# Two transformer blocks on one core: the halves of each buffer of FFN intermediates 1152 bytes apart instead of 1024

## The chip, the cores and the metric

The kernel runs on one core of a Trainium2 chip. The metric is the device time of one execution in microseconds (us), the median of three runs. All sizes in bytes below are bytes within one partition of SBUF, unless something else is said.

## The reference, cut to what matters

The program computes two blocks one after the other on 256 tokens of width 1024, in float32. The first block has two layers. Each layer has two feed-forward networks (FFNs), so there are four: f00, f01, f10 and f11 by their names in the kernel.

```
def swiglu(x, w_gu, w_down):
    gate, up = jnp.split(x @ w_gu, 2, axis=-1)     # w_gu 1024 x 5632, w_down 2816 x 1024
    return (jax.nn.silu(gate) * up) @ w_down

h = h + 0.5 * rmsnorm(swiglu(rmsnorm(h, g[0]), ffn_w_gu[l, 0], ffn_w_down[l, 0]), g[1])
```

Between the FFNs of layer 0 stands a gated convolution, between those of layer 1 a differential attention. The second block has a sparse attention, a state-space branch, and a mixture of 32 experts with 2 chosen for each token. The change touches the first block alone.

## The kernel before, in words

**Float32 products in three matmuls.** Each operand is split into a high part (hi), which ScalarE rounds to TensorE's fast float32 form, and a low part (lo), the rest, which VectorE subtracts. A product is then three matmuls that accumulate in PSUM: hi·hi, hi·lo and lo·hi. Weights come by DMA in units of 512 KB (4096 bytes per partition, tile `raw`), line 170 makes `hi`, line 175 makes `lo`. They lie in nine pairs of slots, a to f and x to z.

**One FFN.** `Ffn.body` (line 613) goes through the 2816 hidden columns in 11 pieces of 256.
- For a piece, `wstat` (line 485) makes the gate `g`, and a second call the up part `u`. Each is 48 matmuls of 256 columns: the weights are stationary and the transposed activations `xTh`, `xTl` are moving. Lines 491, 492 and 493 take turns.
- ScalarE takes silu of `g`, VectorE multiplies by `u`, and `split` (line 400) writes the result as the pair `hTh`, `hTl`. Each of these tiles holds two halves, hidden columns 0 to 127 and 128 to 255 of the piece, 256 tokens each. They come from the pool `hp` with four buffers for the high and four for the low parts.
- `rows` (line 498) then multiplies an older piece by its two units of `w_down`. Here the halves of `hTh` and `hTl` are stationary, 128 tokens at a time, and 512 columns of the weights are moving. The loop is over the halves outside and the token halves inside, so a block is 12 matmuls on half 0 and then 12 on half 1, into four PSUM banks `fo`. Lines 392, 393 and 394 (`mm3`) take turns.

So the steady order on TensorE is 48 matmuls of `g`, 48 of `u`, a block of 24 of `fo`, and again. In f00, f01 and f11 the first two pieces are made token-stationary (`fq`, lines 392 to 394) while the norm of the second token half is still running, and there are blocks at pieces 2 to 8; pieces 9 and 10 have none. In f10 there are blocks at pieces 1 to 7. That is 7 blocks for each FFN. The last four pieces of `fo`, the tail, are multiplied in `boundary` (line 506): for the first token half, for each PSUM bank, piece by piece, both halves in turns of 3 matmuls; for the second token half 6 matmuls for each half.

Other products with 512 moving columns, which the prediction uses for comparison, are `co` and `ao` (the convolution and attention of block one, whose stationary tiles `yT` and `oT` lie in the same pool `hp`), and `wa` and `ws` in block two (stationary tiles `oTh0` to `oTl1`, and `yTh`, `yTl` from other pools). `xb` and `tk` are products of block two in the manner of `g` and `u`, and of `fq`.

**Where the tiles lie.** The allocator of the built program gives these first bytes, and the remainder by 256 in the last column:

| tiles | first byte in a partition | mod 256 |
|---|---|---|
| weights, slots a to f | 56832, and on by 4096 | 0 |
| weights, slots x to z | 168704, and on by 4096 | 0 |
| `xTh`, `xTl` | 212928, 221120 | 192 |
| `hTh`, `hTl`, eight buffers, half 0 | 152320, and on by 2048 | 0 |
| the same, half 1 | 1024 further | 0 |
| `oTh0`, `oTh1`, `oTl0`, `oTl1` (for `wa`) | 140160, and on by 4096 | 128 |
| `yTh` for `ws` (two of four groups) | 111936, 107840 | 64 |
| `yTl` for `ws` (the same groups) | 157440, 136064 | 0, 128 |

All steps inside a weight tile, 1024 or 2048 bytes, and inside `xT`, 1024 bytes, are multiples of 256. So are the steps to the second half of the columns or tokens, 512 bytes. What remains of a tile's first byte is therefore that of every stationary or moving piece taken from it.

The order on each engine is made by a scheduler from the program and its priorities.

Of the kernel before, what the change touches and what calls it, by code (L numbers as in the profile page):

```python
# [9 lines left out]
F32R = mybir.dt.float32r  # L10
# [6 lines left out]
P = 128  # L17
T = 256
# [14 lines left out]
B_Q, B_K, B_IK, B_DT, B_AL, B_LAM, B_DS, B_RT, B_END = 0, 64, 128, 192, 224, 256, 512, 544, 580  # L33

UNIT = 1024
TAIL = 4
CHUNKED = 2
BEHIND = 4
# [38 lines left out]
class Weights:  # L77
# [21 lines left out]
    def raw_of(self, i):  # L99
        k = (i - self.base) % self.nr  # L100
        for pool, n in reversed(self.raws):
            k -= n
            if k < 0:
                break
        return pool.tile([P, UNIT], F32, name=f"raw{i}", tag="raw")

# [41 lines left out]
    def step(self):  # L148
# [7 lines left out]
        self.free.remove(s)  # L156
        hi = self.pools[s].tile([P, UNIT], F32R, name=f"hi{i}", tag=f"hi{s}")
        lo = self.pools[s].tile([P, UNIT], F32R, name=f"lo{i}", tag=f"lo{s}")
        self.slot[i] = s
# [62 lines left out]
def kernel(ctx: ExitStack, tc: tile.TileContext, a: dict, out: bass.AP, upto=99, start=1):  # L222
# [18 lines left out]
    def banks4(name):  # L241
        return [[accp.tile([P, 512], F32, name=f"{name}{i}{j}", tag=f"acc{i}{j}") for j in range(2)] for i in range(2)]
# [5 lines left out]
    def add_piece(w, c0):  # L248
        return [W.add(cols(w, c0, c0 + 256, k, k + 4)) for k in (0, 4)]

    def add_rows(w, k0, n=2):
        return [W.add(cols(w, 0, D, k, k + 1)) for k in range(k0, k0 + n)]

    def add_ffn(l, j, chunked):
        gu, dn = a["ffn_w_gu"][l, j], a["ffn_w_down"][l, j]
        g, u, d = [], [], []
        for n in range(FT // 2):
            g.append(add_piece(gu, n * 256))
            u.append(add_piece(gu, DFF + n * 256))
            if chunked <= n < FT // 2 + chunked - TAIL:  # L260
                d.append(add_rows(dn, 2 * (n - chunked)))
        d += [add_rows(dn, FT - 2 * n) for n in range(TAIL, 0, -1)]
        return g, u, d
# [82 lines left out]
    hp = blk1.enter_context(tc.tile_pool(name="hp", bufs=4))  # L346
# [37 lines left out]
    def scr(name, dt=F32):  # L384
        return sc.tile([P, 512], dt, name=name, tag="sc")


    def hot(n=HOT):
        return tc.high_priority(offset=n)
# [40 lines left out]
    def post_norm(i, acc, g, factor):  # L430
        ss = mean_square(acc[i], D)
        t = two.tile([P, D], F32, name="t", tag="t")
        for j in range(2):
            dve.scalar_tensor_tensor(halves(t)[j], acc[i][j], factor, halves(g)[j], op0=ALU.mult, op1=ALU.mult)
        r = rstd_of(ss[:, 0:1], ss[:, 1:2])
        for j in range(2):
            dve.scalar_tensor_tensor(halves(h[i])[j], halves(t)[j], r, halves(h[i])[j], op0=ALU.mult, op1=ALU.add)
# [68 lines left out]
    def boundary(tail, acc, post, nxt, first=False, pooled=POOLED, at=AT, behind_tr=LEFT):  # L506

        for j in range(2):
            for n, (p, lT) in enumerate(tail):
                m = rows(0, p, lT, acc, first and n == 0, n == len(tail) - 1, js=(j,))  # L510
        with hot():
            post(0)
            nxt.pre(0)
        if BEHIND_PRE:
            W.behind(BEHIND_PRE)
        for u in range(W.split, min(W.split + 16, len(W.src))):
            if (u - W.split) in pooled:
                W.on_pool.add(u)
        W.cut = 2
        late[0] = m  # L520
        left = 2 * len(tail)
        for n, (p, lT) in enumerate(tail):
            for m in range(2):
                rows(1, p, lT, acc, first and n == 0, n == len(tail) - 1, m, m + 1)
                left -= 1
                if left == behind_tr:
                    with hot():
                        late[0] = nxt.tr(0)
                    W.behind(BEHIND)
            W.done(*p, pump=left > behind_tr)  # L530
        late[0] = None
        with hot():
            post(1)
        seen = [0]

        def piece_done():
            seen[0] += 1
            if seen[0] == at:
                with hot():
                    nxt.pre(1)  # L540
                    late[0] = nxt.tr(1)
                W.behind(BEHIND)

        at = nxt.at or at
        hook[0] = piece_done
        nxt.chunk(0)
        hook[0] = late[0] = None
        if seen[0] < at:
            seen[0] = at - 1
            piece_done()  # L550
            late[0] = None
        W.cut = 1
        nxt.chunk(1)
# [30 lines left out]
    class Ffn(Phase):  # L584
# [4 lines left out]
            self.chunked = chunked  # L589

        def new_lT(self):
            t = tuple(hp.tile([P, 2, T], F32R, name=f"hT{p}", tag=f"hT{p}") for p in "hl")
            self.lT.append(t)
            return t

# [17 lines left out]
        def body(self, nxt):  # L613
            x = xT[self.key]
            acc = None
            np_ = FT // 2
            for n in range(self.chunked, np_):
                g_ps = bank("g")
                wstat(x, self.gp[n], g_ps)
                hd = scr("hd")  # L620
                act.activation(hd, g_ps, AF.Silu)
                if n == self.chunked:
                    for q in range(n):
                        self.chunk_end(q)
                u_ps = bank("u")
                wstat(x, self.up[n], u_ps)
                dve.tensor_tensor(out=hd, in0=hd, in1=u_ps, op=ALU.mult)
                lT = self.new_lT()
                split(hd[:, :].rearrange("p (k t) -> p k t", t=T), lT[0], lT[1])
                lag = max(self.chunked, 1)  # L630
                if acc is None and n >= lag:
                    acc = banks4("fo")
                if lag <= n < np_ + lag - TAIL:
                    d = n - lag
                    for m in range(2):
                        for i in range(2):
                            rows(i, self.dp[d], self.lT[d], acc, d == 0, False, m, m + 1)
                    W.done(*self.dp[d])
            boundary(list(zip(self.dp, self.lT))[-TAIL:], acc, lambda i: post_norm(i, acc, gb[self.gout], 0.5), nxt)


    class Conv(Phase):
# [13 lines left out]
        def body(self, nxt):  # L656
            x = xT["cv"]
            bT, lTs, acc = [], [], banks4("co")
            for n in range(4):
                c_ps = bank("c")  # L660
                wstat(x, self.cc[n], c_ps)
                u = scr("u")
                act.activation(u, c_ps, AF.Copy)
                if n % 2 == 0:
                    for b in two_T([self.bs[n // 2, i] for i in range(2)], "bT"):
                        s = scr("bT")
                        act.activation(s, b, AF.Copy)
                        bT.append(s)
                z_ps = bank("z")
                wstat(x, self.cz[n], z_ps)  # L670
                dve.tensor_tensor(out=u, in0=u, in1=z_ps, op=ALU.mult)
                uv = u[:, :].rearrange("p (k t) -> p k t", t=T)
                v = scr("v")
                vv = v[:, :].rearrange("p (k t) -> p k t", t=T)
                for m in range(2):
                    ck = [pcol[:, 1, R2_CK + j * KT + 2 * n + m:R2_CK + j * KT + 2 * n + m + 1] for j in range(3)]
                    dve.tensor_scalar(vv[:, m], uv[:, m], ck[2], None, op0=ALU.mult)
                    for s in (1, 2):
                        dve.scalar_tensor_tensor(vv[:, m, s:], uv[:, m, :T - s], ck[2 - s], vv[:, m, s:], op0=ALU.mult, op1=ALU.add)
                dve.tensor_tensor(out=v, in0=v, in1=bT[n], op=ALU.mult)  # L680
                lT = tuple(hp.tile([P, 2, T], F32R, name=f"yT{p}", tag=f"hT{p}") for p in "hl")
                split(vv, lT[0], lT[1])
                lTs.append(lT)
            boundary(list(zip(self.co, lTs)), acc, lambda i: post_norm(i, acc, gb["03"], 1.0), nxt, True)
# [30 lines left out]
    class DiffAttn(Phase):  # L715
# [18 lines left out]
        def body(self, nxt):  # L734
# [15 lines left out]
            bias, A, R, lTs = {}, {}, {}, {}  # L750
# [63 lines left out]
            def o_t(hd):  # L814
                b = bank("oT")
                os_ = R.pop(hd)
                for i in range(2):
                    pe.transpose(b[:, i * P:(i + 1) * P], os_[:, i * P:(i + 1) * P], ident)
                if hd % 2 == 0:
                    lTs[hd // 2] = tuple(hp.tile([P, 2, T], F32R, name=f"oT{p}", tag=f"hT{p}") for p in "hl")  # L820
                t = lTs[hd // 2]
                split(b[:, :T], t[0][:, hd % 2], t[1][:, hd % 2], subg)

# [585 lines left out]
    class Ring:  # L1409
# [9 lines left out]
        def load(self, n=999):  # L1419
            while n and self.free and self.loaded < len(self.src):  # L1420
                i, (p, tag) = self.loaded, self.free.pop(0)
                t = p.tile([P, UNIT], F32, name=f"mw{i}", tag=tag)
                ap = self.src[i]
# [15 lines left out]
    class Moe(Phase):  # L1439
# [131 lines left out]
        def body(self, _):  # L1571
# [124 lines left out]
            with tc.If(over > 0):  # L1696
# [17 lines left out]
                def owt(ap):  # L1714
                    p, tag = ring_w.free.pop(0)
                    ring_w.free.append((p, tag))
                    wt = p.tile([P, UNIT], F32, name="owt", tag=tag)
                    wv = wt[:, :].rearrange("p (k c) -> p k c", c=256)
# [221 lines left out]
```

## Time and profile before

| | |
|---|---|
| median of 3 runs | 1690.39 us (1684.88 to 1690.99) |
| the profiled execution's own time | 1690.51 us |
| its span | 1688.7 us |
| TensorE busy | 96% of the span |
| VectorE, ScalarE, GpSimd busy | 56%, 47%, 8% |
| bytes read from HBM | 338.22 MB, 201 GB/s over the span |
| granted TensorE clock, mean | 0.988 of full |

The page says that the ends of matmuls are modelled, so that a matmul's own duration says little. How fast TensorE goes is read from starts: the start of one matmul to the start of the next, or a stretch divided by the number of matmuls that start in it. This is called the pace below.

### The profile page before, as it was taken

To read this page: it belongs to the slowest core of one execution; us is meant where nothing else is said; L and a number is where in the kernel's file an instruction comes from. 1 tells how busy PE (TensorE), PEld (TensorE's weight loads), DVE (VectorE), ACT (ScalarE), POOL (GpSimd) and SP (SyncE) were. 2 spreads that over 40 slices of the span, in tenths; PEclk is the share of its full clock that TensorE was granted. 3 is DMA by queue.
4 is the path that set the end of the run, shared out by engine and by line. 5 is a ranking of instruction groups with operands and counts; after the bars stand their busy time and mean duration, and the time that the engine had idled before them with its cause. 6 is when DMAs were issued, how large, how long until landed. Compare 5 with 4: busy or idle time off the path is not lost.

```text
span 1688.7 us, 28506 instructions
## 1 busy us (share of the span) xinstructions
PE 1626.6 (96%) x11550; PEld 1408.9 (83%) x11550; DVE 939.0 (56%) x1429; ACT 785.6 (47%) x1226; POOL 139.5 (8%) x145
## 2 busy tenths in 40 slices
PE   7999999999999999998999999999999997999997
PEld 7999899899989999986899989989989885555543
DVE  5654566754556545477655456967676565232332
ACT  5544454544445444366554445675667643111111
POOL 1000100100010000014200014500222000000000
PEclk9999999999999999999999999999999997999999
DMA  8766474766647566553366645425444755999991
GB/s 287 248 189 187 143 227 130 222 210 188 183 156 228 169 187 193 176 175 94 122 209 191 186 139 168 128 88 165 135 126 126 254 167 209 399 397 388 416 407 71
DMA packets 211655, 341.19 MB, mean 202 GB/s; under 512 B 14612, under 2 KB 166445, under 8 KB 211389
## 3 DMA queue, kind: packets, MB, share of 16 engines
q1 hardware_dynamic: 211485, 339.24, 60.8%
q8 instruction: 92, 1.51, 0.4%
q14 instruction: 46, 0.38, 0.1%
q0 software_dynamic: 32, 0.07, 0.0%
HBM read 338.22 MB, written 1.05 MB: 201 GB/s over the span
## 4 chain that ended last, share of the span: by engine, by line
PE 81%; DVE 7%; ACT 4%; issue 3%; DMA 2%; POOL 1%; SPq 0%; ACTq 0%; POOLq 0%; DVEq 0%
PE eg L1611 7%; PE g L491 4%; PE g L492 4%; PE u L491 4%; PE g L493 4%; PE u L493 4%; PE u L492 4%; PE fo L394 4%; PE fo L393 4%; PE fo L392 4%; PE ey L1634 3%; DVE lo L175 2%; PE sc L1659 2%; PE tk L394 2%; PE tk L393 2%
## 5 line engine op out<-in xcount | busy, mean ns | idle before, releaser
L175 DVE TENSOR_TENSOR lo<-raw,hi 128x1024 fp32r<-128x1024 f32 (+1 forms) x446 | 523.5, 1183 | 385.0 <-ACT hi L170 382.8
L170 ACT ACTIVATE hi<-raw 128x1024 fp32r<-128x1024 f32 (+1 forms) x434 | 456.1, 1057 | 447.8 <-PE g L492 114.7
L491 PE MATMUL g<-xTh_f,hi 128*128 128x256 f32 x608 | 171.6, 282 | 0.0
L492 PE MATMUL g<-xTl_f,hi 128*128 128x256 f32 x608 | 171.5, 282 | 0.0
L491 PE MATMUL u<-xTh_f,hi 128*128 128x256 f32 x608 | 171.3, 282 | 0.0
L493 PE MATMUL g<-xTh_f,lo 128*128 128x256 f32 x608 | 171.3, 282 | 0.0
L492 PE MATMUL u<-xTl_f,hi 128*128 128x256 f32 x608 | 171.0, 281 | 0.0
L493 PE MATMUL u<-xTh_f,lo 128*128 128x256 f32 x608 | 170.9, 281 | 0.0
L392 PE MATMUL fo<-hi,hTh 128*128 128x512 f32 x352 | 137.3, 390 | 0.0
L393 PE MATMUL fo<-lo,hTh 128*128 128x512 f32 x352 | 137.0, 389 | 0.0
L394 PE MATMUL fo<-hi,hTl 128*128 128x512 f32 x352 | 136.3, 389 | 0.0
L493 PEld LDWEIGHTS g<-xTh_f,lo 128*128 128x128 f32 x608 | 117.3, 193 | 0.0
L493 PEld LDWEIGHTS u<-xTh_f,lo 128*128 128x128 f32 x608 | 116.9, 192 | 0.0
L492 PEld LDWEIGHTS g<-xTl_f,hi 128*128 128x128 f32 x608 | 115.1, 189 | 1.4 <-DVE xTl_f L403 0.3
L491 PEld LDWEIGHTS g<-xTh_f,hi 128*128 128x128 f32 x608 | 115.1, 189 | 1.3 <-DVE xTl_f L403 0.3
L491 PEld LDWEIGHTS u<-xTh_f,hi 128*128 128x128 f32 x608 | 114.5, 188 | 0.1
L492 PEld LDWEIGHTS u<-xTl_f,hi 128*128 128x128 f32 x608 | 114.6, 188 | 0.0
L417 POOL TENSOR_TENSOR rstd<-var,mhalf 128x1 f32<-128x1 f32 (+1 forms) x41 | 28.0, 684 | 963.4 <-DVE var L415 911.4
L394 PE MATMUL tk<-hi,xTl_at 128*128 128x256 f32 x320 | 90.6, 283 | 0.0
L393 PE MATMUL tk<-lo,xTh_at 128*128 128x256 f32 x320 | 90.5, 283 | 0.0
L392 PE MATMUL tk<-hi,xTh_at 128*128 128x256 f32 x320 | 90.1, 282 | 0.0
L394 PEld LDWEIGHTS fo<-hi,hTl 128*128 128x128 f32 x352 | 66.1, 188 | 13.7
(475 smaller groups left out, 3534.6 us busy)
## 6 DMA issues: line engine op xcount, KB each, us to landing
raw<-in_ffn_w_gu_dram SPq DMA_DIRECT2D x176, 512.0 KB, 4.5
raw<-in_ffn_w_down_dram SPq DMA_DIRECT2D x88, 512.0 KB, 4.3
raw<-in_w_in_dram SPq DMA_DIRECT2D x72, 512.0 KB, 4.1
mw<-in_w_gate_dram SPq DMA_DIRECT2D x64, 512.0 KB, 7.7
mw<-in_w_up_dram SPq DMA_DIRECT2D x64, 512.0 KB, 7.3
mw<-in_w_down_dram SPq DMA_DIRECT2D x64, 512.0 KB, 7.8
raw<-in_conv_w_in_dram SPq DMA_DIRECT2D x24, 512.0 KB, 4.6
raw<-in_w_kv_dram SPq DMA_DIRECT2D x16, 512.0 KB, 5.6
```

Source lines behind the costliest of these rows:

```text
L170: self.order(self.nc.scalar.activation(hi[:q, :n], r[:q, :n], AF.Copy))
L175: self.order(e.tensor_tensor(out=lo[:q, c:c + cut], in0=r[:q, c:c + cut], in1=hi[:q, c:c + cut].bitcast(F32), op=ALU.subtract))
L392: ms = (pe.matmul(ps, lhsT=xh, rhs=wh, start=first, stop=False), pe.matmul(ps, lhsT=xh, rhs=wl, start=False, stop=False), pe.matmul(ps, lh ...
L393: pe.matmul(ps, lhsT=xh, rhs=wl, start=False, stop=False),
L394: pe.matmul(ps, lhsT=xl, rhs=wh, start=False, stop=last))
L417: pool.tensor_tensor(out=r, in0=v, in1=mhalf[:, :n], op=ALU.pow)
L491: pe.matmul(o, lhsT=wh, rhs=x[0][:, k], start=(k == 0), stop=False)
L492: pe.matmul(o, lhsT=wh, rhs=x[1][:, k], start=False, stop=False)
L493: pe.matmul(o, lhsT=wl, rhs=x[0][:, k], start=False, stop=(k == KT - 1))
L1611: pe.matmul(b[64 * v:64 * v + 64, :T], lhsT=x[:, k], rhs=w[2 * v + k // 4][:, k % 4], start=(k == 0), stop=(k == KT - 1))
L1634: pe.matmul(acc[p][64 * j:64 * j + 64], lhsT=t[:, k], rhs=w[:, j * 512:(j + 1) * 512], start=(e == 0 and k == 0), stop=(e == 1 and k == 1))
L1659: pe.matmul(bs[j], lhsT=t[r, i * P:(i + 1) * P], rhs=y[r, q], start=(q == 0), stop=(q == 1))
```

## The change

The tiles of the pool `hp` grow from 2048 to 2304 bytes. In the FFNs the second half of a tile begins 1152 bytes after the first (256 tokens of 4 bytes and a gap of 32 elements). In the convolution and the attention, which take tiles of the same pool, the halves stay 1024 bytes apart and the rest of the tile is unused.

```
+LT_GAP = 32
...
+    def lT_tile(name, tag, gap=0):
+        t = hp.tile([P, 2 * (T + LT_GAP)], F32R, name=name, tag=tag)
+        return t[:, :2 * (T + gap)].rearrange("p (k t) -> p k t", t=T + gap)[:, :, :T]
...
         def new_lT(self):
-            t = tuple(hp.tile([P, 2, T], F32R, name=f"hT{p}", tag=f"hT{p}") for p in "hl")
+            t = tuple(lT_tile(f"hT{p}", f"hT{p}", LT_GAP) for p in "hl")
...
-                lT = tuple(hp.tile([P, 2, T], F32R, name=f"yT{p}", tag=f"hT{p}") for p in "hl")
+                lT = tuple(lT_tile(f"yT{p}", f"hT{p}") for p in "hl")
...
-                    lTs[hd // 2] = tuple(hp.tile([P, 2, T], F32R, name=f"oT{p}", tag=f"hT{p}") for p in "hl")
+                    lTs[hd // 2] = tuple(lT_tile(f"oT{p}", f"hT{p}") for p in "hl")
```

No instruction is added, removed or moved: all five engines have the same instructions in the same order. The 44 writes of `hTh` on ScalarE and the 44 of `hTl` on VectorE have the shape 128x2x256 instead of 128x512.

In the built program the eight buffers stand at 152320 and on by 2304, so half 0 keeps the remainder 0 by 256, and half 1 of an FFN tile gets the remainder 128. The weight slots x to z move up by 2048 bytes, and keep the remainder 0. All other tiles stay where they were, or are used at other times.

## Rows read from the trace of the kernel before

**Rows 1.** The page: span, busy time of the engines, and tenths in 40 slices.

```profile
span 1688.7 us, 28506 instructions
PE 1626.6 (96%) x11550; PEld 1408.9 (83%) x11550; DVE 939.0 (56%) x1429; ACT 785.6 (47%) x1226; POOL 139.5 (8%) x145
...
PE   7999999999999999998999999999999997999997
...
PEclk9999999999999999999999999999999997999999
```

**Rows 2.** Windows (columns as named): `g`, `u`, `fo` of f00, f01, f10, f11.

```profile
core 0: us, PE busy (x) PEld busy (x) DVE busy (x) ACT busy (x) POOL busy (x), PEclk, DMA share, GB/s
55.78:178.87 123.09, 123.09 (x913) 117.47 (x912) 63.51 (x61) 56.47 (x61) 0.00 (x0) 1.00 0.65 199
344.13:467.22 123.09, 123.09 (x913) 117.47 (x912) 60.64 (x58) 55.00 (x59) 0.00 (x0) 1.00 0.63 190
574.14:708.54 134.40, 134.40 (x1009) 128.78 (x1008) 66.64 (x64) 60.36 (x65) 0.00 (x0) 1.00 0.63 189
862.16:985.25 123.09, 123.09 (x913) 117.47 (x912) 60.64 (x58) 55.00 (x59) 0.00 (x0) 1.00 0.62 189
```

**Rows 3.** Timeline of PE (start, us, instruction): the first block of `fo` in f00.

```profile
50.32 0.39 PE L392 MATMUL fo<-hi,hTh 128*128 128x512 f32 x1
50.55 0.40 PE L393 MATMUL fo<-lo,hTh 128*128 128x512 f32 x1
50.79 0.39 PE L394 MATMUL fo<-hi,hTl 128*128 128x512 f32 x1
51.02 0.39 PE L392 MATMUL fo<-hi,hTh 128*128 128x512 f32 x1
51.24 0.39 PE L393 MATMUL fo<-lo,hTh 128*128 128x512 f32 x1
...
55.78 0.28 PE L491 MATMUL g<-xTh_f,hi 128*128 128x256 f32 x1
```

**Rows 4.** Windows: `g` and `u` of f10 ahead of its first `fo`; `k`.

```profile
557.81:568.68 10.87, 10.87 (x98) 10.87 (x97) 5.95 (x7) 5.37 (x6) 0.00 (x0) 1.00 0.71 209
516.60:533.55 16.95, 16.95 (x146) 16.95 (x145) 10.46 (x9) 10.98 (x13) 0.00 (x0) 1.00 0.93 289
```

**Rows 5.** Windows, instructions of `wa` alone: a stretch of `wa` without a break.

```profile
1166.62:1183.34 16.72, 16.72 (x72) 13.38 (x72) 1.76 (x3) 1.00 0.84 253
```

**Rows 6.** Timeline of PE: from the first stretch of `wa` to `xb`.

```profile
1154.57 0.40 PE L394 MATMUL wa<-hi,oTl 128*128 128x512 f32 x1
1154.80 0.28 PE L491 MATMUL xb<-xTh_at,hi 128*128 128x256 f32 x1
1154.92 0.28 PE L492 MATMUL xb<-xTl_at,hi 128*128 128x256 f32 x1
1155.03 0.28 PE L493 MATMUL xb<-xTh_at,lo 128*128 128x256 f32 x1
...
1155.83 0.28 PE L491 MATMUL xb<-xTh_at,hi 128*128 128x256 f32 x1
```

**Rows 7.** Timeline of PE: three matmuls of `ws` that follow each other.

```profile
1366.83 0.40 PE L392 MATMUL ws<-hi,yTh 128*128 128x512 f32 x1
1367.07 0.39 PE L393 MATMUL ws<-lo,yTh 128*128 128x512 f32 x1
1367.29 0.39 PE L394 MATMUL ws<-hi,yTl 128*128 128x512 f32 x1
1367.52 0.40 PE L392 MATMUL ws<-hi,yTh 128*128 128x512 f32 x1
```

**Rows 8.** Line 402 (ns min/median/max): two forms of ScalarE's split.

```profile
L402 ACT ACTIVATE xTh_f<-xT x16: 578/597/610, 11.2 to 832.1; 128x512 fp32r<-128x512 f32 x16
L402 ACT ACTIVATE hTh<-fqT x6: 588/597/602, 48.7 to 852.4; 128x512 fp32r<-128x512 f32 x6
```

## The prediction

> **What bounds the kernel now.** I read the page first. TensorE is busy 96% of the span, with a nine in nearly every slice and a granted clock at or near full, and no other engine passes 56% [rows 1]. So the time of a stage is the number of its matmuls times their pace. I then cut the four FFNs into windows that hold only `g`, `u` and `fo`, from the `g` behind the first block of `fo` to the tail [rows 2]. There TensorE has no idle time at all, the clock is full throughout, VectorE and ScalarE are busy about half the time and DMA 0.62 to 0.65. Nothing but the pace itself can be gained or lost in these 503.67 us, and weights come fast enough for a quicker pace.
>
> The pace comes from the timeline. Within a block of `fo`, from 51.02 to the `g` at 55.78, 21 matmuls start in 4.76 us: 226.7 ns each [rows 3]. The window of f00 then holds 16 x 48 = 768 matmuls of `g` and `u` and 6 x 24 = 144 of `fo` (912; the row counts one more that crosses the edge). 123.09 - 144 x 0.2267 = 90.45 us, over 768: 117.8 ns. f01 and f11 have the same window, and f10 with 18 x 48 = 864 gives (134.40 - 32.64) / 864 = 117.8 ns too [rows 2].
>
> The same instruction can go faster. In f10, ahead of the first `fo`, 96 matmuls of `g` and `u` take 10.87 us: 113.2 ns, half of the 226.7 for half the columns, while DMA is busier (0.71) and ScalarE and VectorE as busy as later [rows 4]. In `k` the slow pace stands again: 144 in 16.95 us, 117.7 ns [rows 4]. So there are two paces, 4.5 ns apart. Neither the clock, nor the other engines, nor the weight slots (all nine take turns in the windows) part them. What does is what went before: once `fo` has run, all of `g` and `u` is slow until the next stall.
>
> `fo` itself shows the change-over. Its first three matmuls behind the fast `u` take 50.32 to 51.02, 0.70 us or 233 ns each, and then it settles at 226.7 [rows 3]. I read this as two ways in which a matmul's moving stream and the load of the next weights, which runs beside it (PEld is busy 117.47 of the 123.09 us, rows 2), can lie against each other. In one, `fo` is at its best and `g`, `u` at their worst; in the other it is the reverse. `fo` pulls the engine into the first, and there it stays.
>
> **What the distance of the addresses has to do with it.** Take the first byte of the next stationary piece less that of the moving piece, by 256. It is 0 in `fo`. Elsewhere it is not, and 512-column matmuls are slower there without idle time: 128 in `wa`, 72 matmuls in 16.72 us, 232.2 ns [rows 5]; in `ws` 0.24 us where the next piece is 64 off, and 0.22 where it is 128 off [rows 7]. `wa` never settles, and the `xb` behind it, a product like `g`, leaves it fast: 0.12, 0.11, and then 7 matmuls from 1155.03 to 1155.83, 114 ns each [rows 6]. So a distance of 0 is what locks the engine, and a distance of 128 doesn't.
>
> **The change part by part.** Half 1 of each FFN tile moves from distance 0 to 128, the distance of `wa`. Half 0 stays at 0. In each body block 12 matmuls on half 0 come first, then 12 on half 1, then `g`.
>
> Gain: behind half 1, `g` should do what `xb` does behind `wa`: two or three slow matmuls and then the fast pace through `g` and `u`. 3 x 768 + 864 = 3168 matmuls by 4.5 ns are 14.3 us. Each of the 28 runs of `g` and `u` (7 an FFN) enters slowly, at some 0.01 us [rows 6]: 0.3 us. 14.0 us are left.
>
> Cost in the blocks: each now comes out of a fast `u`, so its first three matmuls take 0.70 instead of 0.68 us, 0.02 x 28 = 0.6 us [rows 3]. Half 1 goes at the pace of `wa`: 5.5 ns x 12 x 28 = 1.8 us [rows 5]. Where 128 comes singly, as in `ws`, a matmul takes 0.22 us, at `fo`'s own pace [rows 7], and then this term is nothing; or at `ws`'s 0.24 it would be 13 x 336 = 4.4 us. I take `wa`, in which all matmuls have this distance.
>
> Cost in the tails: 96 matmuls an FFN, with the halves in turns of three or six. If no turn settles, all 384 cost 5.5 ns, 2.1 us; if only half 1 does, 1.05 us. I take 1.0, since half 0 settles after three in rows 3.
>
> ScalarE's and VectorE's 44 writes each get a gap in the middle. `xTh_f` is written in four pieces 1024 bytes apart and has the median of the unbroken `hTh` from PSUM, 597 ns both [rows 8]. So I cost them at nothing, between -10 and +10 ns each. Were there a cost, TensorE would not see it: in the body the piece multiplied is an older one, and ScalarE is idle for half of the window [rows 2].
>
> Sum: -14.0 + 0.6 + 1.8 + 1.0 = -10.6 us. No stage of the FFNs waits for anything else, and what follows starts earlier by as much. The profiled execution took 1690.51 us, 0.12 over the median of the runs, so I set the forecast at 1680 us.
>
> One thing I leave out of the sum. The products behind a tail can flip too. `k` is slow now [rows 4], and with the products before it and those behind f00's and f11's tails there are about 1100 such matmuls: up to 4.5 x 1100 = 4.9 us more, or nothing, since stalls stand between.
>
> The Trainium skill speaks against all of this. "SBUF — State Buffer", section "Who interferes with whom", gives TensorE two independent read ports, one for the moving operand and one for the weight load, and says that TensorE never waits on anyone. By that rule no address matters and the sum is 0. Rows 2 to 5, with 226.7 and 232.2 or 113.2 and 117.8 ns for the same instruction, do not agree.
>
> **The rivals.**
> - *Nothing happens.* Half 1 stays in the lock that half 0 has just made. `wa` never stood behind a distance of 0, so no row shows that step; 12 matmuls may be too few, and the 0.22 us at 128 in `ws` is `fo`'s own pace [rows 7]. Then `g` is as slow as now: 1690.5 us. Against it: in 72 matmuls `wa` never settles [rows 5]. This is also where the page's rule would end.
> - *Half of it.* `g` is freed only behind some blocks, or falls back at the change to `u`: 7 us of gain less 3.3 of cost, 1687 us. Against it: in f10 the fast pace goes on from `g` to `u` [rows 4].
> - *Slower.* `fo` loses its lock for both halves and `g` does not gain. The place is the 672 body matmuls and the 384 of the tails: by `wa` 1056 x 5.5 = 5.8 us, 1696 us; by the 0.24 of `ws` 1056 x 13 = 13.7 us, 1704 us [rows 5, 7]. It decides if half 0 does not settle within its 12 matmuls. Rows 3 speak against it: it took three.
>
> **How the numbers follow.** The forecast has 0.58, with a range of its own of 1675 to 1684: costs between 0.6 + 0 + 1.0 and 0.6 + 4.4 + 2.1 put it at 1678 to 1683.6, and the products behind the tails reach down to 1675. Nothing happens 0.24, half of it 0.10, slower 0.08. The range to 1692 takes in the two cases near the old time, with what the runs scatter; the slower case and little else is left out, and below I leave 1674. What a measurement can tell from no change is about 0.5%, 8.5 us: 1682 and 1699. Of the forecast most lies below 1682, about 0.53, and nothing of the others but 0.01. Of the slower case a little more than half is over 1699, 0.05. The rest, 0.41, is within.
>
> **What the profile would show.** Right: in the four windows `g` and `u` at 113.2 ns after the first two or three, so that a window of 123.09 us becomes about 120; `fo` with its first three at 233 ns, the next nine at 226.7, and half 1 near 232; ScalarE's split still about 600 ns. Wrong: half 1 at 226.7 and `g` at 117.8 (the lock holds); half 1 slower and `g` still at 117.8 (the lock is no matter of the last distance before `g`); or a fast `g` that TensorE cannot use, shown by idle time before `hi` or `lo` in the body.

## The result, and the profile after

Both kernels were timed six times on the same chip. The changed kernel takes 1676.84 us (median, 1676.36 to 1684.40), the kernel before 1690.57 us (1684.88 to 1695.35). The ratio is 0.9929 with a 95% interval of 0.9904 to 0.9953, or 13.7 us less. The forecast was 1680, with a range of 1674 to 1692.

The profiled execution of the changed kernel took 1676.58 us, that of before 1690.51. The page of the changed kernel, with the rows that answer to [rows 1]:

```profile
span 1674.8 us, 28506 instructions
PE 1612.4 (96%) x11550; PEld 1390.4 (83%) x11550; DVE 939.2 (56%) x1429; ACT 786.6 (47%) x1226; POOL 139.7 (8%) x145
...
PEclk9999999999999999999999999999999997999998
```

The span is 13.9 us shorter and PE's busy time 14.2 us, with the same instructions. VectorE, ScalarE and GpSimd do what they did. So the same matmuls took less time.

The windows of the four FFN bodies, cut as in [rows 2] (same columns: us, then busy time and count of PE, PEld, DVE, ACT, POOL, then clock, DMA share, GB/s):

```profile
55.94:176.26 120.32, 120.32 (x913) 114.18 (x912) 63.71 (x62) 56.76 (x61) 0.00 (x0) 1.00 0.67 204
339.89:460.22 120.33, 120.33 (x914) 114.20 (x912) 60.60 (x58) 55.07 (x59) 0.00 (x0) 1.00 0.63 193
565.19:696.40 131.21, 131.21 (x1009) 125.07 (x1008) 66.60 (x64) 60.42 (x65) 0.00 (x0) 1.00 0.63 194
848.40:968.73 120.33, 120.33 (x913) 114.19 (x912) 60.59 (x58) 55.05 (x59) 0.00 (x0) 1.00 0.63 193
```

The reader is to see that TensorE still has no idle time and the full clock, that the counts are the same, and that each window is 2.8 us shorter, f10's 3.2: 11.5 us in all. By starts, `g` and `u` went from 117.8 to 113.4 ns a matmul in the mean, and `fo` in the windows from 226.7 to 230.7.

The timeline of PE (start, us, instruction) at the first block of `fo` in f00, where [rows 3] stood:

```profile
50.40 0.39 PE L398 MATMUL fo<-hi,hTh 128*128 128x512 f32 x1
50.63 0.40 PE L399 MATMUL fo<-lo,hTh 128*128 128x512 f32 x1
50.86 0.39 PE L400 MATMUL fo<-hi,hTl 128*128 128x512 f32 x1
51.09 0.39 PE L398 MATMUL fo<-hi,hTh 128*128 128x512 f32 x1
...
53.14 0.40 PE L398 MATMUL fo<-hi,hTh 128*128 128x512 f32 x1
...
55.94 0.28 PE L497 MATMUL g<-xTh_f,hi 128*128 128x256 f32 x1
56.05 0.28 PE L498 MATMUL g<-xTl_f,hi 128*128 128x256 f32 x1
56.17 0.28 PE L499 MATMUL g<-xTh_f,lo 128*128 128x256 f32 x1
56.28 0.28 PE L497 MATMUL g<-xTh_f,hi 128*128 128x256 f32 x1
```

Half 0 takes 50.40 to 53.14, 228 ns each with the slow first three; half 1 takes 53.14 to 55.94, 2.80 us for 12, 233 ns each; and `g` behind it needs 0.34 us for its first three. In these hundredths a slow entry can't be seen. By the trace's starts in ns, in the mean of the 28 runs of `g` behind a block, the first three matmuls take 120, 116 and 114 ns, and from the fourth on each takes 113.3.

ScalarE's split (ns, minimum/median/maximum), where [rows 8] stood; the lines of the kernel have moved by six:

```profile
L408 ACT ACTIVATE hTh<-hd x38: 632/635/637, 56.1 to 970.5; 128x512 fp32r<-128x512 f32 x38
L408 ACT ACTIVATE hTh<-fqT x6: 579/594/602, 49.0 to 838.5; 128x512 fp32r<-128x512 f32 x6
```

The gap in the written tile costs nothing: the median of the second form was 597 ns before.

**Where the rest of the time went.** Four stretches outside the windows, first in the kernel before (the tail of f00, the convolution's `c` and `z`, and f10 and f11 from their start to their first `fo`), with a fifth row that cuts out of f10's the stretch in which the clock was low:

```profile
178.87:201.53 22.66, 22.66 (x106) 18.86 (x105) 12.56 (x17) 9.41 (x16) 4.31 (x4) 1.00 0.18 56
230.12:277.20 47.08, 47.08 (x400) 47.08 (x401) 32.47 (x49) 23.29 (x28) 0.00 (x0) 1.00 0.68 208
543.24:568.68 25.44, 25.42 (x194) 24.88 (x193) 10.22 (x12) 9.64 (x11) 0.00 (x0) 0.87 0.49 145
819.61:856.72 37.11, 37.11 (x307) 37.11 (x306) 24.90 (x32) 20.85 (x28) 4.60 (x5) 0.95 0.70 225
543.30:550.10 6.80, 6.78 (x30) 6.24 (x30) 1.58 (x3) 0.60 (x1) 0.00 (x0) 0.50 0.36 116
```

and then the first four in the changed kernel:

```profile
176.26:199.36 23.10, 23.10 (x107) 18.89 (x106) 12.82 (x17) 9.41 (x16) 4.33 (x4) 1.00 0.20 60
227.47:272.90 45.43, 45.43 (x401) 45.43 (x401) 32.14 (x49) 23.34 (x28) 0.00 (x0) 1.00 0.67 209
536.89:559.66 22.77, 22.43 (x195) 22.03 (x193) 10.24 (x12) 9.64 (x11) 0.00 (x0) 1.00 0.53 163
807.04:842.88 35.84, 35.84 (x308) 35.63 (x305) 24.76 (x32) 20.86 (x28) 4.62 (x5) 1.00 0.72 232
```

Each tail is 0.43 to 0.44 us longer, 1.74 in four. The four first blocks are 0.36 us longer together. With the windows that is -11.5 + 1.74 + 0.36 = -9.4 us from the new addresses in the FFNs.

`c` and `z` went at the fast pace, 1.65 us less. That is not shown to be the change's work. The same stretch in experiment 1, whose FFNs go at the paces of before, and in experiment 11, whose `g` and `u` go at that of the changed kernel:

```profile
230.06:275.49 45.43, 45.43 (x401) 45.43 (x401) 32.13 (x49) 23.34 (x28) 0.00 (x0) 1.00 0.67 214
227.58:274.66 47.08, 47.08 (x400) 47.08 (x401) 32.47 (x49) 23.30 (x28) 0.00 (x0) 1.00 0.67 205
```

Experiment 1 has every distance of before and is fast here; experiment 11 is slow. TensorE stands still for 1.5 us (before) and 1.28 us (experiment 1) ahead of the first `c`, and no run shows what sets the pace after that.

The head of f10 is 2.67 us shorter and that of f11 1.27: in the kernel before the granted clock stood for 6.8 us of f10's head at its lower level, 1.2 of 2.4 GHz, and in this execution of the changed kernel it did not. Behind the tail of f11 the changed kernel is 16.1 us ahead, and 16.5 us where the experts' stage begins. It loses some of that where the experts of the second block are routed, a stretch that both kernels run at the lower level, before and after the change:

```profile
1406.90:1427.40 20.50, 11.29 (x54) 10.36 (x54) 13.91 (x57) 5.36 (x8) 0.55 (x1) 0.50 0.32 127
```

```profile
1389.50:1413.40 23.90, 14.63 (x68) 13.54 (x69) 15.28 (x59) 6.37 (x11) 0.55 (x1) 0.50 0.33 128
```

It takes 3.4 us longer at half clock, with 14 matmuls more in it. Behind it 15.1 us are left, and the span ends 13.9 us shorter.

That the heads of f10 and f11 stay at full clock is not shown to be the change's work. In the 10 us ahead of f10's head TensorE was busy alike, 7.70 of 9.75 us before and 7.94 of 9.99 after, and the clock fell in the one and not in the other. Experiment 1, whose paces are those of before, and experiment 11, whose paces are those of the changed kernel, both have 3.4 us at half clock near this place.

What the windows, the tails and the first blocks explain is 9.4 us. The interval of the ratio reaches from 7.9 to 16.2 us less, which holds it.

How much of the rest is the clock's can be read from the mean granted clock of each run. The kernel before ran 69 more times beside the experiments. At mean clocks of 0.988, 0.989 and 0.990 it took 1690.0, 1688.0 and 1687.9 us on average (24, 10 and 4 runs). Of the changed kernel's six runs one was at 0.988, one at 0.989 and three at 0.990: 1678.84, 1677.10, and 1676.36 to 1676.58 us. That is some 11 us less at the same clock (the sixth, at 0.986, is 8.5 less). So 2 to 3 of the 13.7 us come from a higher clock in these six runs. That this is luck is likely: experiment 3, with the same fast `g` and `u`, had a mean clock of 0.9874 over its runs, and the kernel before beside it 0.9872.

### The profile page after: what moved, and what is told of

It is laid out like the page before. It is cut to its first block, busy times and chain, and to the rows that moved or that the text cites. A ratio compares the mean times of both kernels' runs of the same rounds, so it can differ in the third digit from the quotient of the medians.

```text
span 1674.8 us, 28506 instructions
## 1 busy us (share of the span) xinstructions
PE 1612.4 (96%) x11550; PEld 1390.4 (83%) x11550; DVE 939.2 (56%) x1429; ACT 786.6 (47%) x1226; POOL 139.7 (8%) x145
## 4 chain that ended last, share of the span: by engine, by line
PE 81%; DVE 8%; ACT 4%; issue 3%; DMA 2%; POOL 1%; SPq 0%; ACTq 0%; POOLq 0%; DVEq 0%
PE eg L1617 7%; PE g L498 4%; PE u L499 4%; PE u L498 4%; PE g L497 4%; PE g L499 4%; PE u L497 4%; PE fo L400 4%; PE fo L398 4%; PE fo L399 4%; PE ey L1640 3%; DVE lo L176 2%; PE sc L1665 2%; PE tk L400 2%; PE tk L399 2%
## 5 line engine op out<-in xcount | busy, mean ns | idle before, releaser
L498 PE MATMUL g<-xTl_f,hi 128*128 128x256 f32 x608 | 168.1, 276 | 0.2 <-DVE xTl_f L409 0.2
L497 PE MATMUL g<-xTh_f,hi 128*128 128x256 f32 x608 | 168.2, 277 | 0.1
L499 PE MATMUL g<-xTh_f,lo 128*128 128x256 f32 x608 | 167.9, 276 | 0.0
```

The lines of the kernel that those rows point to most:

```text
L497: pe.matmul(o, lhsT=wh, rhs=x[0][:, k], start=(k == 0), stop=False)
L498: pe.matmul(o, lhsT=wh, rhs=x[1][:, k], start=False, stop=False)
L499: pe.matmul(o, lhsT=wl, rhs=x[0][:, k], start=False, stop=(k == KT - 1))
```

## The experiments

Each kernel was timed together with the kernel before on one chip; the ratio is to that. "Distance" and "pace" are used as in the prediction; "locked" and "free" stand for the slow and the fast pace of `g` and `u` behind a block of `fo`. If nothing else is said, the window shown is that of f00 (123.09 us before, 120.32 after).

**1. The gap without the distance.** The tiles keep their 2304 bytes and the writes their gap, but half 1 begins 1280 bytes after half 0, so that its distance is 0 again.

```diff
-        return t[:, :2 * (T + gap)].rearrange("p (k t) -> p k t", t=T + gap)[:, :, :T]
+        v = t[:, :2 * (T + gap)].rearrange("p (k t) -> p k t", t=T + gap)[:, :, :T]
+        if gap:
+            p_, k_, t_ = v.ap
+            v = bass.AP(tensor=v.tensor, offset=v.offset, ap=[p_, [T + 2 * gap, 2], t_])
+        return v
```

> Half 1 of an FFN tile begins 1280 bytes after half 0, in tiles of the same 2304 bytes; the writes keep the shape 128x2x256, and everything else lies as in the changed kernel. By the theory (what counts is the distance of the next stationary piece from the moving one by 256, which is 0 again) g and u are slow, 117.8 ns, and fo is at 226.7: windows of 123.1, 123.1, 134.4 and 123.1 us as before, the whole near 1690 us. By the rival (the gap, the new write shape or the moved tiles as such do it) g and u stay at 113.4 ns, windows of 120.3 and 131.2 us, the whole near 1677 us.

Measured: 1688.84 us, ratio 0.9996 (0.9984 to 1.0008).

```profile
55.63:178.72 123.09, 123.09 (x913) 117.47 (x912) 62.75 (x61) 55.81 (x60) 0.00 (x0) 1.00 0.65 196
```

To a hundredth of a us this is the window of before. For the FFN windows the gap, the size of the tiles and the shape of the writes do nothing; the address by 256 does all of it.

**2. Half 0 at distance 128, half 1 at 0.**

```diff
-        return t[:, :2 * (T + gap)].rearrange("p (k t) -> p k t", t=T + gap)[:, :, :T]
+        if gap:
+            return t.rearrange("p (k t) -> p k t", t=T + gap)[:, :, gap:]
+        return t[:, :2 * T].rearrange("p (k t) -> p k t", t=T)
```

> Half 0 of an FFN tile at distance 128, half 1 at distance 0, the opposite of the changed kernel. By the theory it is the last distance before g that counts: half 1 settles at 226.7 ns after three matmuls, g and u are slow, 117.8 ns. A window is then 768 x 0.1178 + 6 x (12 x 0.2323 + 3 x 0.232 + 9 x 0.2267) = 123.6 us, the whole near 1694 us with dearer tails. By the rival (any distance of 128 inside a block frees the engine) g and u are at 113.4 ns and a window is 120.3 us, the whole near 1677 us.

Measured: 1691.96 us, 1.0009 (0.9997 to 1.0022). `fo` 229.1 ns, `g` and `u` 117.8.

```profile
56.01:179.47 123.46, 123.46 (x914) 117.51 (x912) 61.90 (x60) 55.00 (x59) 0.00 (x0) 1.00 0.64 195
```

The price in `fo` is paid and nothing is gained. Twelve matmuls at 0 between the ones at 128 and `g` lock the engine again. Between 0 and 128 it is the last half of the block that decides.

**3. Both halves at 128.**

```diff
-        return t[:, :2 * (T + gap)].rearrange("p (k t) -> p k t", t=T + gap)[:, :, :T]
+        return t[:, gap:gap + 2 * T].rearrange("p (k t) -> p k t", t=T)
```

> Both halves of an FFN tile at distance 128 (a contiguous tile of 2048 bytes that begins 128 bytes later). By the theory nothing locks any more: g and u at 113.4 ns, all of fo near 232 ns like wa, a window of 768 x 0.1134 + 144 x 0.2323 = 120.5 us, the whole near 1678 us. By the rival (it is the step from 0 to 128 inside a block that frees g, or a lock can form at 128 as it does at 0) fo settles below 228 ns or g stays at 117.8 ns: a window of 119.8 or of 123.9 us.

Measured: 1679.98 us, 0.9939 (0.9925 to 0.9954). `g` and `u` 113.4 ns, `fo` 232.3, the pace of `wa` in [rows 5].

```profile
55.40:175.97 120.57, 120.57 (x913) 114.23 (x912) 63.33 (x61) 56.37 (x61) 0.00 (x0) 1.00 0.66 203
```

Half 0 may lie at 128 too, for the same gain and 0.25 us more in a window.

**4 and 5. Half 1 64 or 192 bytes off.** One constant changes. The tiles shrink to 2176 bytes or grow to 2432, so every second buffer begins at 128 and the blocks alternate: distances (0, 64) and (128, 192) for the two halves in the first kernel, (0, 192) and (128, 64) in the second. The tiles of the convolution and the attention, from the same pool, begin at 128 in every second buffer too, so the whole times hold that as well.

```diff
-LT_GAP = 32
+LT_GAP = 16     # 4: half 1 64 bytes off
+LT_GAP = 48     # 5: half 1 192 bytes off
```

> The changed kernel with a gap of 64 bytes: half 1 of an FFN tile at distance 64 from the weights. By the theory any distance but 0 ends the lock of fo: g and u near 113.4 ns, half 1 by the ws rows (0.24 us where the next piece is 64 off) near 235 ns, a window of 768 x 0.1134 + 6 x (12 x 0.2283 + 12 x 0.235) = 120.4 us, the whole near 1677 us. By the rival (128 is special, and at 64 fo leaves the engine in the state that makes g slow) g and u stay at 117.8 ns, a window of 124 us, the whole near 1695 us.

> The changed kernel with a gap of 192 bytes: half 1 of an FFN tile at distance 192 from the weights. By the theory any distance but 0 ends the lock of fo: g and u near 113.4 ns, half 1 between 227 and 235 ns, a window of 119.9 to 120.4 us, the whole near 1677 us. By the rival (128 is special) g and u stay at 117.8 ns, a window of 123.1 to 124 us, the whole near 1692 us.

Measured: 1688.90 us, 0.9989 (0.9974 to 1.0004), and 1693.64 us, 1.0019 (1.0003 to 1.0034). Since the blocks differ, the rows below are single runs of 96 matmuls of `g` and `u`. In the fourth kernel behind (0, 64) and behind (128, 192):

```profile
55.72:67.03 11.31, 11.31 (x97) 11.30 (x96) 6.78 (x7) 6.18 (x7) 0.00 (x0) 1.00 0.85 264
72.58:83.48 10.90, 10.90 (x98) 10.90 (x96) 3.81 (x4) 4.73 (x5) 0.00 (x0) 1.00 0.66 194
```

in the fifth behind (0, 192) and behind (128, 64):

```profile
54.19:65.50 11.31, 11.31 (x98) 11.31 (x97) 6.40 (x7) 5.80 (x7) 0.00 (x0) 1.00 0.84 265
71.07:82.37 11.30, 11.30 (x97) 11.30 (x96) 3.86 (x4) 4.73 (x5) 0.00 (x0) 1.00 0.64 198
```

Only the second row is fast: 10.90 us, as in [rows 4]. My reading "any distance but 0 frees" falls. Behind a half at 0, neither 64 nor 192 frees; behind a half at 128, 192 keeps the engine free and 64 locks it.

**6, 7 and 8. The other operand.** The kernel before, with `xTh` and `xTl` moved down by 192, 64 and 128 bytes. `hTh` and `hTl` stay as they were before the change. The distance of `g` and `u` (stationary weights at 0, moving `xT`) goes from 64 to 0, 128 and 192; that of `fq` from 192 to 0, 128 and 64. Everything that lies below `xT` on that side of SBUF moves by the same bytes, among it tiles of the attentions and the experts' weights `mw` of block two. So the FFN windows are what these three are read by, and the whole times hold more than one distance.

```diff
-    ...tile([P, 8], F32, name="even_xt")
+    ...tile([P, 56], F32, name="even_xt")     # 6: distance 0
+    ...tile([P, 24], F32, name="even_xt")     # 7: distance 128
+    ...tile([P, 40], F32, name="even_xt")     # 8: distance 192
```

> The kernel before with xTh and xTl 192 bytes lower, so that their distance from the weights is 0 as well: fo, g, u, fq, c, z, k, tk and xb all have distance 0, and the FFN tiles are as before. By the theory a distance of 0 locks and costs nothing: g and u near 113.3 ns, fo at 226.7, windows of 119.7 and 130.6 us, no dearer tails, and c, z, k, tk near 113 ns too; the whole near 1668 us. By the rival (256 columns and 512 columns cannot both be at their best in one state, whatever the distance) g and u stay at 117.8 ns and the time near 1690 us.

> The kernel before with xTh and xTl 64 bytes lower: distance of g, u and fq 128, fo at 0 as before. If a distance of 128 is bad for 256 columns as it is for 512 (232 against 226.7 ns), g and u are near 119 ns all the time, a window of 124 us, the whole near 1700 us. If each distance has its own best state and that of 128 at 256 columns is the one that fo leaves behind, g and u are at 113.3 ns with fo at 226.7, a window of 119.7 us and cheap tails: the whole near 1672 us.

> The kernel before with xTh and xTl 128 bytes lower: distance of g and u 192, of fq 64, fo at 0 as before; 64 and 192 change places. If the two are alike (as the paces of g at 64 and of fq at 192, 113.3 or 117.8 ns, suggest) g and u go slowly at 117.8 ns behind fo, windows of 123.1 us, the whole near 1690 us. If the state that fo leaves suits 192 and not 64, g and u are at 113.3 ns, a window of 119.7 us, the whole near 1675 us.

Measured: 1704.50 us, 1.0098 (1.0072 to 1.0125); 1703.58 us, 1.0074 (1.0047 to 1.0100); 1691.37 us, 1.0002 (0.9986 to 1.0017). The windows, of the sixth, the seventh and the eighth kernel:

```profile
56.72:181.64 124.92, 124.92 (x914) 119.18 (x913) 63.04 (x61) 56.06 (x61) 0.00 (x0) 1.00 0.65 196
```

```profile
56.62:181.65 125.03, 125.03 (x913) 119.15 (x912) 62.02 (x60) 55.17 (x60) 0.00 (x0) 1.00 0.63 193
```

```profile
55.16:178.49 123.33, 123.33 (x913) 117.49 (x912) 63.20 (x61) 56.32 (x61) 0.00 (x0) 1.00 0.65 198
```

That 0 is a good distance for every width was wrong by the sign: with 256 columns, 0 and 128 give a third pace, 119.9 and 120.0 ns, and give about the same in `c`, `z`, `k`, `cb` and `xb`, where `xT` is an operand too. At 192, `g` and `u` go at 117.8, the slow one of the two paces known so far.

**9 and 10. One of the two tiles only.** The gap stands in `hTl` alone, then in `hTh` alone. A block takes `hTh`, `hTh`, `hTl` in turns, so half 1 has the distances 0, 0, 128, or 128, 128, 0.

```diff
-            t = tuple(lT_tile(f"hT{p}", f"hT{p}", LT_GAP) for p in "hl")
+            t = tuple(lT_tile(f"hT{p}", f"hT{p}", LT_GAP if p == "l" else 0) for p in "hl")   # 9; 10: p == "h"
```

> The changed kernel with the gap in hTl alone: of the 12 matmuls on half 1 only the 4 during which a piece of hTl is loaded see a distance of 128, the others 0. If a few matmuls at 128 are enough to end the lock, g and u are at 113.4 ns and fo is cheaper than now: a window of 120.0 us, the whole near 1675 us. If the matmuls at 0 in between make the lock anew, g and u are at 117.8 ns, a window of 123.2 to 123.5 us, the whole near 1691 us.

> The changed kernel with the gap in hTh alone: of each three matmuls on half 1, the two during which a piece of hTh is loaded see a distance of 128, the third 0. If more matmuls at 128 than at 0 are enough, g and u are at 113.4 ns, a window of 120.2 us, the whole near 1676 us. If every third matmul at 0 holds the lock, g and u are at 117.8 ns, a window of 123.4 us, the whole near 1692 us.

Measured: 1692.66 us, 1.0016 (1.0005 to 1.0026), and 1693.96 us, 1.0031 (1.0019 to 1.0044). `g` and `u` 117.8 ns in both. The windows, of the ninth and the tenth kernel:

```profile
54.95:178.36 123.41, 123.41 (x913) 117.59 (x912) 63.61 (x61) 56.48 (x61) 0.00 (x0) 1.00 0.65 199
```

```profile
56.00:179.65 123.65, 123.65 (x913) 117.52 (x912) 62.25 (x60) 55.35 (x60) 0.00 (x0) 1.00 0.64 196
```

In the ninth the very last stationary piece ahead of `g` lies at 128, and `g` is slow all the same. A single matmul at 128 between two at 0 doesn't free the engine, nor do two of three. Both kernels pay for it in `fo` (228.9 and 230.6 ns) without a gain.

**11. The tail left as before.** The gap stands in the first seven pieces of each FFN, and not in the last four, which the tail multiplies.

```diff
+            t = tuple(lT_tile(f"hT{p}", f"hT{p}", LT_GAP if len(self.lT) < FT // 2 - TAIL else 0) for p in "hl")
```

> The changed kernel, but the last four pieces of each FFN, those of the tail, have no gap, since no g follows them. By the theory the windows stay at 120.3 and 131.2 us, and each tail goes back from 23.09 to 22.66 us: 4 x 0.43 = 1.7 us less, near 1675 us. By the rival (a tail that starts from the fast state pays for it whatever its distances) the tails stay near 23 us and the time near 1677 us.

Measured: 1675.04 us (1674.72 to 1679.48), ratio 0.9916 (0.9903 to 0.9930). The window of f00, the tail behind it, and the head of f10:

```profile
55.98:176.31 120.33, 120.33 (x913) 114.20 (x912) 62.38 (x61) 55.32 (x60) 0.00 (x0) 1.00 0.65 200
176.31:198.98 22.67, 22.67 (x106) 18.87 (x105) 12.62 (x17) 9.41 (x16) 4.32 (x4) 1.00 0.19 58
...
538.60:562.94 24.34, 24.00 (x194) 23.60 (x193) 10.24 (x12) 9.64 (x11) 0.00 (x0) 0.93 0.48 153
```

The window keeps its gain and the tail has its old 22.67 us. This version has the lowest median. It can't be told from the changed kernel by it, since the intervals overlap; the 1.7 us of the tails are shown by the profile alone. The third row is its head of f10, at a mean clock of 0.93.

## Why the prediction was right, and where it was not

- *The bound.* Right. TensorE never idles in the windows, before or after, and what the pace gives the span gets.
- *Gain in `g` and `u`.* Forecast 14.3 less 0.3 for slow entries. Measured 3168 x 4.36 ns = 13.8 us. The entry is there as forecast: the first three `g` behind a block take 10 ns more than three settled ones, 0.3 us in 28 runs. The settled pace is 113.3 ns, where the prediction read 113.2 from [rows 4], and with the entries the mean is 113.4.
- *Cost in the blocks.* Forecast 0.6 + 1.8 = 2.4 us. Measured 576 x 4.02 ns = 2.3 us in the windows, and 0.36 in the first blocks: 2.7. Half 0 settles within its 12 matmuls as [rows 3] had it, and half 1 goes at 233 ns, where `wa` had 232 [rows 5]. That `wa` was the right neighbour, and `ws` [rows 7] not, is settled by experiment 3, where all of `fo` has its pace. The prediction read too much from the hundredths of [rows 7]: its third row, 64 off as well, has 0.23 and not 0.24, and the 0.22 at 128 is 228 ns by the trace's starts, not `fo`'s own 226.7.
- *Cost in the tails.* Mis-sized: 1.0 us forecast, 1.74 measured, nearer to the 2.1 that I gave for a tail in which no turn settles. It is 4.5 ns on each of the 384 matmuls. Half 0, which the forecast put at nothing, pays too: 4.1 ns a matmul in the turns of three, where it does not settle, and 2.1 in the turns of six.
- *Writes.* Nothing, as forecast.
- *The sum.* -9.4 us from these terms, where I had -10.6. The time came out 3 us under the forecast, for what lies outside the sum. At an equal clock the gain is some 11 us, close to the sum; that the medians lie further apart comes from the clock and is no merit of the prediction. In the profiled executions it shows as half-clock stretches in the heads of f10 and f11, where 4 us were saved, that only the one of before has; I had not thought of that. The part that I had left out knowingly, products behind a tail that flip, is open: `c` and `z` were faster by 1.65 us, but experiment 1 has that without the change, and `k`, which I had named, stayed at 117.8.
- *The rivals.* That half 1 stays in the lock, and half of it, are out by the windows. The slower case was nearer for `fo` in the tails, and failed on the gain; experiments 2, 5, 9 and 10, which pay for `fo` and gain nothing, show what it would have looked like, 1.0009 to 1.0031.
- *The reason given.* Half right. That the distance by 256 decides, and that of 0 and 128 the one in the last half ahead of `g` counts, stands (experiments 1 and 2). With 192 in the last half it is half 0 that decides: 128 there is fast, 0 slow (4, 5). That 0 alone locks and anything else frees does not (4, 5), nor that one piece at 128 at the end is enough (9). What the runs support is narrower: a run of matmuls all at 128 frees the engine; pieces at 0 or 64 behind it lock it, 192 doesn't. Why is open; no row of the profile names what TensorE waits for between two matmuls, and the two ways in which stream and load lie against each other were argued, not shown. Nor is it shown that the difference of the two addresses counts: in all these products the weights lie at 0 by 256, so the remainder of the other operand alone would give the same results. Distances of 64 or 192 in both halves, and runs at 128 shorter than 12, were not tried.
- What the prediction drew from the Trainium skill ("SBUF — State Buffer", section "Who interferes with whom", two independent read ports of TensorE), that no address matters, does not hold here: experiment 1 and the changed kernel differ in the address of half 1 alone, and the same matmuls take 123.09 and 120.32 us. No run shows whether it is the ports that collide.

## What to carry to other kernels

Where TensorE is busy without a break, divide a stretch by its matmuls and see whether one instruction has more than one pace at the same clock; if so, the addresses of the stationary and the moving tile, by 256 bytes, are worth a trial, since a few unused bytes in a tile were worth some 0.7% here. Such a pace can outlast the instructions that set it, so look at the group that ran before the slow one, not only at the slow one. Try the distances on the chip instead of extending a rule from one case: of the eleven other layouts here only two were faster than before, and one guess was wrong by its sign.

## What the runs showed of the hardware

- A float32 matmul of 512 moving columns takes 226.7 ns at full clock in a settled run with stationary and moving pieces a multiple of 256 bytes apart, and 232.3 ns at 128 (experiment 3).
- With 256 columns there are three paces: 113.3 and 117.8 ns at a distance of 64, by what ran before, and 119.9 at 0 and 120.0 at 128 in the FFN windows.
- The share of time that the clock is granted in full differs between executions of one kernel: mean clocks of 0.985 to 0.991 in 69 runs of the kernel before, and 1692.9 us on average at 0.986 against 1687.9 at 0.990.
- The pace survives hundreds of matmuls: `g` and `u` keep their pace through 96 of them until the next `fo`, and `c` and `z` through some 400, slow in the kernel before and fast in experiment 1 at the same distances (47.08 and 45.43 us above).
